# A four-layer decoder trunk: where the first layer's shift and scale vectors are made, and where its squares are summed

## The chip, the cores and the metric

The kernel runs on one core of a Trainium2 chip. The metric is the device time of one execution in microseconds (us); the lower the better. The core has five engines that run side by side, each with its own instruction queue: TensorE (PE, matmuls, with a queue of weight loads shown as PEld), VectorE (DVE), ScalarE (ACT), GpSimd (POOL) and SyncE (SP, which issues most of the transfers). Transfers run on 16 DMA engines.

## The reference

The input x has 256 tokens of 1024 features. Four layers follow each other; each has a token mixer (layer 0: sliding-window attention with 16 query heads and 4 key heads) and a SwiGLU feed-forward part. Ahead of each part x is normed and modulated by vectors that are made from one conditioning vector c:

```python
c_act = jax.nn.silu(c)
for i in range(DEPTH):
    mod = c_act @ ada_w[i] + ada_b[i]          # 1024 -> 6 * 1024
    sh1, sc1, g1, sh2, sc2, g2 = jnp.split(mod, 6, axis=-1)
    h = modulate(rmsnorm(x, norm_gain[i, 0]), sh1, sc1)   # norm * (1 + scale) + shift
    y = swa_mixer(h, ...)                      # by layer: swa, gla, fox, swa
    x = x + g1[:, None, :] * y
    h = modulate(rmsnorm(x, norm_gain[i, 1]), sh2, sc2)
    x = x + g2[:, None, :] * swiglu(h, ffn_w_gu[i], ffn_w_down[i])
return rmsnorm(x, final_norm)
```

So a layer has six vectors of 1024 values, each the product of silu(c) with a 1024 x 1024 matrix of float32. For layer 0 the first two, shift and scale, are needed before anything else can begin.

## The kernel before

x lies with its features on the partitions: 8 tiles k of 128 features by 256 tokens. All matrices are float32. A weight is split into a high and a low part (wh by a cast on ScalarE, L195; wl by a subtraction on VectorE, L197), and so is the normed input (hh, hl). A product of the two is three matmuls (`mm3`, L258): high by high, high by low, low by high.

**The stream of loads.** `items` (L1131) writes one list of all weight transfers, about 1 MB each: "w" items are weights, "a" items are pairs of 128-row tiles of a conditioning matrix. `Stream` (L76) walks it in order. Five raw buffers exist (`RAW`); the transfer of an item is put on SP's queue as soon as the item five places ahead is done, and waits there until the buffer is free. An item is done in two pieces each (`piece`, L99). For layer 0 the order is written out by hand in `ORDER0` (L56): w a weight of the attention, h the shift, s the scale, g the gate of the attention, H and S shift and scale of the feed-forward part, in pairs of tiles. It begins w s h s h s h h w s.

**The conditioning vectors.** `ada_pieces` (L201) makes one tile of 128 values per piece. The matrix lies with outputs on the partitions and the 1024 inputs in a row, and `cact` holds silu(c) on all partitions. One VectorE instruction multiplies, sums along the row and adds the bias (L217). For the tiles that `POOL_ADA` (L60) names, GpSimd multiplies (L212), ScalarE sums the row (L214), and VectorE adds the bias (L215). In layer 0 these are 18 tiles: 5 of the shift, 1 of the scale, 3 of the gate, 5 and 4 of the feed-forward part's shift and scale.

**The first norm.** `first_chunks` (L682) begins layer 0. ScalarE squares the 8 tiles of x (L405), GpSimd adds them up (L416), and a matmul with a column of 1/1024 sums over the partitions (`stat_start` and `stat_end`, L305 to L326; the last tile goes in separately), then the root on ScalarE and the reciprocal y on VectorE (L326). `spread` (L328) puts y onto all partitions, copied as rbs (L694). Then four rounds r follow. Each forces the pairs r of shift and scale, makes A = (1 + scale) * gain (L361), and two tiles of the normed input (`h_tiles`, L426): tk on VectorE (L435), hh on ScalarE with the shift as bias (L437), hl on VectorE (L430). As soon as a weight is ready, the matmuls of the chunk run over the tiles that exist. Chunk 0 (keys, in the PSUM banks "mm") and chunk 1 (values, in the banks "s") are made like this. The value chunk is copied as v by ScalarE (L732), the keys get their rotary position on VectorE (L609 to L612) and GpSimd (L618).

**Behind it.** `swa` (L718) makes four query chunks while a generator, `attn_heads` (L529), is stepped beside them: scores on PE (L544, L545), mask and minimum on VectorE (L572), exponentials on ScalarE (L577), division on ScalarE and VectorE (L557, L558), transposes (L585), the product with the values (L551, L552). GpSimd copies two sink columns for each head (L569, L570). Then comes the output projection and the feed-forward part.

The program's instructions are put into each engine's queue by a scheduler, which keeps the order of the data and may put a later independent instruction ahead of one that it expects to wait.

Of the kernel before, what the change touches and what calls it, by code (L numbers as in the profile page):

```python
# [17 lines left out]
P = 128  # L18
# [16 lines left out]
    ("fin", KT), ("hnorm", 2), ("bgate", GH), ("bf", 1),  # L35
# [20 lines left out]
ORDER0 = "wshshshhwswwwgwwgggSwHSwHSSHHw"  # L56
# [3 lines left out]
POOL_ADA = {(0, 0): (0, 1, 2, 4, 5), (0, 1): (7,), (0, 2): (1, 3, 4), (0, 3): (0, 1, 2, 4, 5), (0, 4): (1, 3, 4, 7)}  # L60
# [83 lines left out]
class Builder:  # L144
# [56 lines left out]
    def ada_pieces(self, it, raw):  # L201

        nc = self.nc
        layer, nt = it[1]
        mod = self.mod[layer]
        bias = self.c("ada_b")[:, layer * 48:(layer + 1) * 48]

        def piece(i):
            w = raw[:, i * D:(i + 1) * D]
            col, b = mod[:, nt + i:nt + i + 1], bias[:, nt + i:nt + i + 1]  # L210
            if (nt + i) % KT in POOL_ADA.get((layer, nt // KT), ()):
                nc.gpsimd.tensor_tensor(out=w, in0=w, in1=self.cact, op=ALU.mult)  # L212
                s = self.t(self.small, [P, 1], "adac", bufs=2)
                nc.scalar.activation(w, w, AF.Copy, accum_out=s)  # L214
                nc.vector.tensor_tensor(out=col, in0=s, in1=b, op=ALU.add)  # L215
            else:
                nc.vector.tensor_tensor_reduce(out=w, in0=w, in1=self.cact, scale=1.0, scalar=b,  # L217
                                               op0=ALU.mult, op1=ALU.add, accum_out=col)
        return [lambda: piece(0), lambda: piece(1)]

# [460 lines left out]

    def first_chunks(self):  # L682

        nc = self.nc
        self.A, self.late = None, []
        self.st.cap = self.st.widx[EARLY]
        self.per_tick = 0.0
        for k in range(KT):
            self.x_done(k)
        self.stat_start(self.acc)  # L690
        self.stat_end()
# [7 lines left out]
        for r in range(4):  # L699
            self.st.force_ada(0, (0, 1), r)  # L700
            self.mod_cols(0, 0, 2 * r, 2 * r + 2, A)
            self.h_tiles(range(2 * r, 2 * r + 2), rbs, A, sh, hh, hl)
            while len(ws) < EARLY and (r == 3 or self.st.pos[f"i0_{len(ws)}"] < self.st.done):
                c = len(ws)
                ws.append([x.rearrange("p (k n) -> p k n", k=KT) for x in self.st.get(f"i0_{c}")])
                self.st.cap = self.st.widx[EARLY]
                outs.append(self.banks(("mm", "s")[c])[0])
                todo.append(0)
            for c, (wh, wl) in enumerate(ws):
                for k in range(todo[c], 2 * r + 2):  # L710
                    for m in range(2):
                        sl = slice(m * P, (m + 1) * P)
                        self.mm3(outs[c][m][:, :S], hh[:, k, sl], hl[:, k, sl], wh[:, k], wl[:, k],
                                 k == 0, k == KT - 1)
                todo[c] = 2 * r + 2
# [483 lines left out]
    def build(self):  # L1199
# [24 lines left out]
        for i in range(2):  # L1224
            ps = self.ps("t")
            sl = slice(i * 512, (i + 1) * 512)
            nc.tensor.matmul(ps, one, crow[:, sl], start=True, stop=True)
            nc.scalar.activation(self.cact[:, sl], ps, AF.Silu)

# [47 lines left out]
def _layout(i):  # L1277
# [5 lines left out]
    a["ada"] = ada.reshape(DEPTH * 6, 4, 2, P, D).transpose(0, 1, 3, 2, 4).reshape(DEPTH * 6, 4, P, 2 * D)  # L1283
    gu = i["ffn_w_gu"].reshape(DEPTH, KT, P, 2, FT, P)[:, :, :, :, :2]
# [30 lines left out]
    put("ones", np.tile(np.array([[1.0 / D, 1.0 / 256]], f), (P, 1)))  # L1315
    put("eps", np.full((P, 1), EPS, f))
# [44 lines left out]
```

## Time and profile before

| | |
|---|---|
| median of 3 runs | 1285.93 us (1284.1 to 1291.37) |
| profiled execution | 1287.15 us, span 1285.4 us |
| PE busy in the span | 1223.3 us (95%) |
| VectorE busy | 1029.2 us (80%) |
| ScalarE busy | 719.4 us (56%) |
| GpSimd busy | 200.5 us (16%) |
| DMA | 298.50 MB, mean 232 GB/s |

The span runs from the first to the last instruction of the program. A row of the view in order of time has start and length in us, engine, line, operation, what is written and read, the shape and a count; brackets give how long the engine was idle before it, and which instruction ended that. A row of the groups has the count, busy time in us and mean in ns of one, then idle time. A row of the waits has the total in us, the number of waits, and the longest. A row of the busy time by stage has the stage, its length, each engine's busy time with its count, the granted clock of TensorE (PEclk), the share of the DMA engines and GB/s.

### The profile page before, as it was taken

How to read it: one execution, taken by the hardware profiler on the slowest of the kernel's cores; microseconds unless marked ns; L12 is line 12 of the kernel's file. 1: busy time of each engine (PE TensorE's matmuls, PEld its weight loads, DVE VectorE, ACT ScalarE, POOL GpSimd, SP SyncE). 2: the span in 40 equal slices, each digit the busy share in tenths (PEclk: the TensorE clock that was granted, in tenths of full speed). 3: DMA queues.
4: the chain of work that ended last, by engine and by line, in shares of the span. 5: the costliest groups of instructions: out<-in, count | busy, mean ns of one | idle time of the engine just before them, and what ended most of it. 6: DMA issues, size and time to landing. Idle time of an engine off the chain costs nothing.

```text
span 1285.4 us, 19492 instructions
## 1 busy us (share of the span) xinstructions
PE 1223.3 (95%) x7284; PEld 1061.3 (83%) x7284; DVE 1029.2 (80%) x1839; ACT 719.4 (56%) x1323; POOL 200.5 (16%) x211
## 2 busy tenths in 40 slices
PE   3698999999999999999999999999999999999997
PEld 2676888888898998888899889888889878888886
DVE  5999998878779889888877657988787977766553
ACT  4567764444576665444448766644445667644442
POOL 5468110001105321000120101100011012000011
PEclk9999999999999999999999999999999999999999
DMA  8665779977744436997875443799777434665450
GB/s 328 256 231 196 267 290 358 340 262 266 264 161 167 165 132 231 352 340 279 271 280 210 157 170 109 275 357 336 273 266 257 168 128 139 222 214 202 161 176 33
DMA packets 44673, 298.50 MB, mean 232 GB/s; under 512 B 5169, under 2 KB 5329, under 8 KB 14242
## 3 DMA queue, kind: packets, MB, share of 16 engines
q1 hardware_dynamic: 43778, 295.53, 63.7%
q8 instruction: 57, 0.93, 0.3%
q10 hardware_dynamic: 432, 1.20, 0.2%
q0 software_dynamic: 368, 0.53, 0.1%
q14 instruction: 38, 0.31, 0.1%
HBM read 296.15 MB, written 1.05 MB: 231 GB/s over the span
## 4 chain that ended last, share of the span: by engine, by line
PE 83%; DVE 9%; ACT 3%; issue 2%; DMA 2%; POOL 1%; DVEq 0%; SPq 0%; POOLq 0%; ACTq 0%
PE mm L1100 13%; PE mm L260 12%; PE mm L261 11%; PE mm L262 11%; PE mm L1102 7%; PE s L260 6%; PE s L261 6%; PE s L262 6%; DVE raw L217 2%; DVE wl L197 2%; PE o L551 2%; PE t L1071 1%; PE s L545 1%; DMA raw<-in_ada 1%; PE t L585 1%
## 5 line engine op out<-in xcount | busy, mean ns | idle before, releaser
L197 DVE TENSOR_TENSOR wl<-raw,wh 128x1024 fp32r<-128x1024 f32 (+2 forms) x408 | 454.6, 1147 | 85.5 <-ACT wh L195 84.3
L195 ACT CAST wh<-raw 128x1024 fp32r<-128x1024 f32 (+2 forms) x408 | 376.5, 963 | 224.2 <-issue 105.9
L1100 PE MATMUL mm<-a,wh 128*128 128x512 f32 x704 | 248.8, 395 | 0.0
L217 DVE CUSTOM_DVE_ANT_0 raw<-raw,cact,const 128x1024 f32<-128x1024 f32 x174 | 230.0, 1337 | 15.3 <-DMA raw<-in_ada 15.3
L260 PE MATMUL mm<-wh,hh 128*128 128x512 f32 (+1 forms) x560 | 200.5, 358 | 20.1 <-ACT hh L437 20.1
L1102 PE MATMUL mm<-a,wl 128*128 128x256 f32 x704 | 199.5, 283 | 0.0
L262 PE MATMUL mm<-wh,hl 128*128 128x512 f32 (+1 forms) x560 | 195.5, 350 | 1.3 <-DVE hl L430 1.3
L261 PE MATMUL mm<-wl,hh 128*128 128x512 f32 (+1 forms) x560 | 195.4, 349 | 0.0
L416 POOL TENSOR_TENSOR sq<-sq,sq 128x256 f32<-128x256 f32 x54 | 59.7, 1105 | 751.2 <-ACT sq L405 731.8
L1100 PEld LDWEIGHTS mm<-a,wh 128*128 128x128 f32 x704 | 132.4, 188 | 29.7
L260 PE MATMUL s<-wh,hh 128*128 128x512 f32 (+2 forms) x384 | 144.7, 378 | 2.9 <-ACT hh L437 2.9
L261 PE MATMUL s<-wl,hh 128*128 128x512 f32 (+2 forms) x384 | 143.0, 373 | 0.2 <-DVE wl L197 0.2
L262 PE MATMUL s<-wh,hl 128*128 128x512 f32 (+2 forms) x384 | 142.2, 374 | 0.0
L260 PEld LDWEIGHTS mm<-wh,hh 128*128 128x128 f32 x560 | 108.4, 194 | 36.2 <-ACT hh L437 21.0
L1102 PEld LDWEIGHTS mm<-a,wl 128*128 128x128 f32 x704 | 132.8, 189 | 0.2
L262 PEld LDWEIGHTS mm<-wh,hl 128*128 128x128 f32 x560 | 107.6, 193 | 14.9 <-DVE hl L430 2.0
L261 PEld LDWEIGHTS mm<-wl,hh 128*128 128x128 f32 x560 | 108.4, 194 | 12.5 <-issue 0.7
L497 DVE SCALAR_TENSOR_TENSOR x<-mm,mod,x 128x256 f32<-128x256 f32 x128 | 61.2, 481 | 44.5 <-PE mm L1102 35.4
L260 PEld LDWEIGHTS s<-wh,hh 128*128 128x128 f32 x384 | 72.5, 189 | 15.3 <-ACT hh L437 3.4
L261 PEld LDWEIGHTS s<-wl,hh 128*128 128x128 f32 x384 | 72.3, 188 | 12.4 <-DVE wl L197 0.5
L262 PEld LDWEIGHTS s<-wh,hl 128*128 128x128 f32 x384 | 71.7, 188 | 12.8
L260 PE MATMUL mm<-oh,wh 128*128 128x256 f32 x256 | 74.7, 297 | 2.6 <-DVE x L497 2.5
(223 smaller groups left out, 2154.6 us busy)
## 6 DMA issues: line engine op xcount, KB each, us to landing
raw<-in_ada SPq DMA_DIRECT2D x96, 1024.0 KB, 6.8
raw<-in_gu SPq DMA_DIRECT2D x88, 1024.0 KB, 6.5
raw<-in_down SPq DMA_DIRECT2D x64, 704.0 KB, 4.9
raw<-in_swa_in SPq DMA_DIRECT2D x12, 1024.0 KB, 5.1
raw<-in_gla_in SPq DMA_DIRECT2D x11, 1024.0 KB, 6.9
raw<-in_fox_in SPq DMA_DIRECT2D x11, 1024.0 KB, 5.3
raw<-in_swa_o SPq DMA_DIRECT2D x8, 1024.0 KB, 5.0
raw<-in_gla_o SPq DMA_DIRECT2D x4, 1024.0 KB, 4.8
```

Of the source, the lines that this page charges most:

```text
L195: nc.scalar.copy(wh[:, sl], raw[:, sl])
L197: eng.tensor_tensor(out=wl[:, sl], in0=raw[:, sl], in1=wh[:, sl].bitcast(F32), op=ALU.subtract)
L217: nc.vector.tensor_tensor_reduce(out=w, in0=w, in1=self.cact, scale=1.0, scalar=b, op0=ALU.mult, op1=ALU.add, accum_out=col)
L260: nc.tensor.matmul(out, ah, bh, start=first, stop=False)
L261: nc.tensor.matmul(out, ah, bl, start=False, stop=False)
L262: nc.tensor.matmul(out, al, bh, start=False, stop=last)
L416: (eng or nc.gpsimd).tensor_tensor(out=q, in0=self.acc, in1=q, op=ALU.add)
L497: self.nc.vector.scalar_tensor_tensor(out=self.x[:, m], in0=ps, scalar=gate[:, m:m + 1], in1=self.x[:, m], op0=ALU.mult, op1=ALU.add)
L545: nc.tensor.matmul(sc[:, P:3 * P], q[:, P:], k, start=True, stop=True)
L551: nc.tensor.matmul(o[rows, :S], v[0], pt[:, :S], start=True, stop=False)
L1100: nc.tensor.matmul(o, wh[:, k], a[:, kk].rearrange("p e n -> p (e n)"), start=kk == 0, stop=False)
L1102: nc.tensor.matmul(o[:, S:], wl[:, k], a[:, kk, 0], start=False, stop=kk == FT - 1)
```

## The change

The shift vector of layer 0's first norm is made by TensorE: the first 1024 columns of `ada_w[0]` lie in memory with the inputs on the partitions, two tiles of outputs per transfer, as before 1 MB each. Eight accumulating matmuls with silu(c) as columns (`ccol`, new, made by eight matmuls and one activation at the start) give one row of 256 values in PSUM; ScalarE copies it, two small matmuls turn it into two columns, and VectorE adds the bias (`ada_rows`). The turn is queued when the round's scale tiles have been queued. All other conditioning vectors are made by VectorE alone, so that the 18 products of GpSimd and their sums on ScalarE are gone. The squares of x are no longer added on GpSimd: PE takes the sum over partitions of every square and adds it up in PSUM (`stat_all`). The list of loads begins h s w h s h s w h s in place of w s h s h s h h w s, and the first weight is taken up in round 0.

```diff
-    ("fin", KT), ("hnorm", 2), ("bgate", GH), ("bf", 1),
+    ("fin", KT), ("hnorm", 2), ("bgate", GH), ("bf", 1), ("one", 1),
...
-ORDER0 = "wshshshhwswwwgwwgggSwHSwHSSHHw"
+ORDER0 = "hswhshswhswwwgwwgggSwHSwHSSHHw"
...
-POOL_ADA = {(0, 0): (0, 1, 2, 4, 5), (0, 1): (7,), (0, 2): (1, 3, 4), (0, 3): (0, 1, 2, 4, 5), (0, 4): (1, 3, 4, 7)}
...
+        if layer == 0 and nt < KT:
+            return self.ada_rows(mod[:, nt:nt + 2], bias[:, nt:nt + 2], raw)
+
         def piece(i):
             w = raw[:, i * D:(i + 1) * D]
             col, b = mod[:, nt + i:nt + i + 1], bias[:, nt + i:nt + i + 1]
-            if (nt + i) % KT in POOL_ADA.get((layer, nt // KT), ()):
-                nc.gpsimd.tensor_tensor(out=w, in0=w, in1=self.cact, op=ALU.mult)
-                s = self.t(self.small, [P, 1], "adac", bufs=2)
-                nc.scalar.activation(w, w, AF.Copy, accum_out=s)
-                nc.vector.tensor_tensor(out=col, in0=s, in1=b, op=ALU.add)
-            else:
-                nc.vector.tensor_tensor_reduce(out=w, in0=w, in1=self.cact, scale=1.0, scalar=b,
-                                               op0=ALU.mult, op1=ALU.add, accum_out=col)
+            nc.vector.tensor_tensor_reduce(out=w, in0=w, in1=self.cact, scale=1.0, scalar=b,
+                                           op0=ALU.mult, op1=ALU.add, accum_out=col)
         return [lambda: piece(0), lambda: piece(1)]
+
+    def ada_rows(self, mod, bias, raw):
+
+        nc = self.nc
+        w = raw[:, :2048].rearrange("p (k n) -> p k n", k=KT)
+        ps = self.ps("o")
+        row = self.t(self.small, [P, S], "fc", bufs=2)[:1]
+
+        def product():
+            for k in range(KT):
+                nc.tensor.matmul(ps[:1, :S], self.ccol[:, k:k + 1], w[:, k], start=k == 0, stop=k == KT - 1)
+            nc.scalar.copy(row, ps[:1, :S])
+
+        def turn():
+            for m in range(2):
+                nc.tensor.matmul(ps[:, S + m:S + m + 1], row[:, m * P:(m + 1) * P], self.c("one")[:1],
+                                 start=True, stop=True)
+            nc.vector.tensor_tensor(out=mod, in0=ps[:, S:S + 2], in1=bias, op=ALU.add)
+        return [product, lambda: self.turns.append(turn)]
...
+    def stat_all(self):
+
+        nc = self.nc
+        self.stat = [self.ps("t"), self.ps("t")]
+        for k in range(KT):
+            q = self.t(self.small, [P, S], "sq", bufs=4)
+            nc.scalar.activation(q, self.x[:, k], AF.Square)
+            if k == KT - 1:
+                self.last_sq = q
+                break
+            for b in range(NB):
+                nc.tensor.matmul(self.stat[b][:, :1], q[:, b * P:(b + 1) * P],
+                                 self.c("ones")[:, 0:1], start=k == 0, stop=False)
+        self.stat_end()
+
     def first_chunks(self):
 
         nc = self.nc
-        self.A, self.late = None, []
         self.st.cap = self.st.widx[EARLY]
         self.per_tick = 0.0
-        for k in range(KT):
-            self.x_done(k)
-        self.stat_start(self.acc)
-        self.stat_end()
+        self.turns = []
+        self.stat_all()
...
             self.st.force_ada(0, (0, 1), r)
+            self.turns.pop()()
             self.mod_cols(0, 0, 2 * r, 2 * r + 2, A)
             self.h_tiles(range(2 * r, 2 * r + 2), rbs, A, sh, hh, hl)
-            while len(ws) < EARLY and (r == 3 or self.st.pos[f"i0_{len(ws)}"] < self.st.done):
+            while len(ws) < EARLY and (r % 3 == 0 or self.st.pos[f"i0_{len(ws)}"] < self.st.done):
                 c = len(ws)
+                if r == 0 and c:
+                    break
...
+        ps = self.ps("o")
+        for k in range(KT):
+            nc.tensor.matmul(ps[:, k:k + 1], crow[:, k * P:(k + 1) * P], one[:, :1], start=True, stop=True)
+        self.ccol = self.t(self.small, [P, KT], "ccol", bufs=1)
+        nc.scalar.activation(self.ccol, ps[:, :KT], AF.Silu)
...
+    a["ada"][0] = _chunks(i["ada_w"][0, :, :D], 256)
...
+    put("one", np.ones((P, 1), f))
```

The tag "o" has one PSUM bank, the tag "fc" two buffers, "sq" four.

## The prediction

> **What bounds the kernel now.** I read the busy time by stage first, then the waits and the chain of the first 55 us, then the rows in order of time there, then the groups of the stage behind it. Only layer 0 is touched: 0 to 55 us makes its first norm and two projection chunks, 55 to 145 us holds its attention and output projection, the rest is untouched.
>
> ```profile
> core 0: us, PE busy (x) PEld busy (x) DVE busy (x) ACT busy (x) POOL busy (x), PEclk, DMA share, GB/s
> 0.00:55.00 55.00, 23.92 (x112) 19.38 (x113) 38.40 (x59) 23.47 (x42) 24.97 (x22) 1.00 0.79 302
> 55.00:145.00 90.00, 81.43 (x533) 65.36 (x532) 87.90 (x196) 64.97 (x160) 53.69 (x51) 0.97 0.61 226
> 145.00:1285.00 1140.00, 1117.99 (x6644) 976.51 (x6643) 902.93 (x1586) 630.96 (x1123) 121.81 (x140) 0.99 0.64 229
> ```
>
> PE is busy for 1118.0 of the last 1140 us, but idle for 31.1 of the first 55 us and 8.6 of the next 90 us: those two numbers cap what this change can win. In the first stage VectorE works 38.4 us and does hardly anything before 14.87 us, so it has no room left there.
>
> ```profile
> by line: DVE raw L217 28.8%; DMA raw<-in_ada 16.1%; issue 10.2%; DMA x<-in_x 10.0%; DVE hl L430 8.3%; POOL sq L416 7.1%; DVE wl L197 6.5%; DVE A L361 4.5%; DVE tk L435 4.1%; PE t L309 1.8%; PE t L322 1.6%; ACT sq L405 1.3%; ACT hh L437 0.9%
> PE mm L260 <- ACT hh L437: 20.1, 3, 9.0
> 14.62 5.63 POOL L212 TENSOR_TENSOR raw<-raw,cact 128x1024 f32<-128x1024 f32 x2 [2.00 <-DMA raw<-in_ada]
> 14.87 0.17 DVE L326 RECIPROCAL y<-sd 128x2 f32<-128x2 f32 x1 [13.88 <-ACT sd L325]
> 15.01 3.04 DVE L217 CUSTOM_DVE_ANT_0 raw<-raw,cact,const 128x1024 f32<-128x1024 f32 x1
> 17.97 3.36 DVE L217 CUSTOM_DVE_ANT_0 raw<-raw,cact,const 128x1024 f32<-128x1024 f32 x1
> 24.66 1.28 DVE L217 CUSTOM_DVE_ANT_0 raw<-raw,cact,const 128x1024 f32<-128x1024 f32 x1
> 50.26 0.16 DVE L215 TENSOR_TENSOR mod<-adac,const 128x1 f32<-128x1 f32 x1
> 51.72 0.89 DVE L430 SCALAR_TENSOR_TENSOR hl<-tk,mod,hh 128x256 fp32r<-128x256 f32 x2 [0.18 <-ACT hh L437]
> 54.96 0.37 ACT L732 COPY v<-s 128x256 f32<-128x256 f32 x1 [0.99 <-PE s L262]
> ```
>
> The first line is the chain's share by line up to 55 us: the adaLN products on VectorE (L217) lead it, and PE waits 20.1 us for the normed tiles hh. The rows below say why. A product of 1024 columns costs VectorE 1.28 us alone (24.66) and 3.04 to 3.36 us while GpSimd runs its own (14.62 to 20.25): the two engines do not run such operations at once, one stands until the other is through. So the work given to GpSimd is not free to VectorE. The last shift column is there at 50.42 us and the last low half hl at 52.61 us; the second chunk's copy v starts at 54.96 us. I measure the first stage by these two ends.
>
> **The change, first stage: VectorE's own list.**
>
> ```profile
> L217 DVE CUSTOM_DVE_ANT_0 raw<-raw,cact,const 128x1024 f32<-128x1024 f32 x10 | 20.6, 2079 | 0.0
> L197 DVE TENSOR_TENSOR wl<-raw,wh 128x1024 fp32r<-128x1024 f32 x4 | 4.7, 1218 | 0.0
> L435 DVE SCALAR_TENSOR_TENSOR tk<-rbs,A,x 128x256 f32<-128x256 f32 x8 | 3.5, 482 | 0.1
> ```
>
> The groups of the first 55 us: ten products at 2079 ns become eight at 1.28 us (all scale tiles; tile 7 comes over from GpSimd, shift tiles 3, 6 and 7 go to PE): 10.2 us. The rest stays: splits 4.7, tk 3.5, hl 8 x 0.44 = 3.5 (from the 51.72 row), four A and four shift additions at 0.16 = 1.3. That is 23.2 us. From 14.87 us without a wait it ends at 38.1 us.
>
> Loads. The shift and scale vectors with the two weight chunks are ten transfers of 1 MB, in five buffers.
>
> ```profile
> 1.56 5.50 DMA x<-in_x
> GB/s 0 93 231 407 441 417 435 411 429 429 423 429 411 412 273 0 149 399 435 393 429 423 125 334 375 209 411 131 0 0 0 71 340 429 405 369 292 357 346 411
> const<-in_const ACTq DMA_DIRECT2D x1, 656.0 KB, 6.6
> ```
>
> At the full slices' 420 to 430 GB/s 1.05 MB takes 2.45 us. Behind x (7.06 us), ten of them and the second constants (1.6 us) end at 33.2 us; two products (2.56) and what follows the last column now (50.26 to 52.61, 2.35) end at 38.1 us. The row also shows slices at 0 between 38 and 43 us: the queue stood there for a buffer. The new order puts shift 0 ahead of scale 0 ahead of weight 0; every queue behind SP's is in that order, and a buffer whose product is late holds all later loads. No other queue gains or loses a load.
>
> PE's new list: per round of two shift tiles, 8 matmuls of 256 columns into one row, two turns of the row into columns; per square, two matmuls; eight matmuls for the column form of c.
>
> ```profile
> 3.27 0.33 PEld L1227 LDWEIGHTS t<-hh,fc 1*128 1x128 f32 x1 [0.52 <-issue]
> 4.12 0.33 PEld L1227 LDWEIGHTS t<-hh,fc 1*128 1x128 f32 x1 [0.52 <-issue]
> 2.28 3.75 PE L1227 MATMUL t<-hh,fc 1*128 1x512 f32 x4 [2.28 <-DMA hh<-in_c]
> 12.68 1.01 PE L309 MATMUL t<-const,sq 128*128 128x1 f32 x4 [6.65 <-POOL sq L416]
> 13.55 0.99 PE L322 MATMUL t<-const,sq 128*128 128x1 f32 x4
> 15.09 1.22 PE L332 MATMUL t<-const,y 128*128 128x128 f32 x4 [0.55 <-DVE y L326]
> 154.90 0.61 PE L309 MATMUL t<-const,sq 128*128 128x1 f32 x4 [0.60 <-POOL sq L416]
> 73.80 0.43 PE s L545 x2
> 37.81 0.42 PE L261 MATMUL mm<-wl,hh 128*128 128x256 f32 x1
> 38.03 0.42 PE L260 MATMUL mm<-wh,hh 128*128 128x256 f32 x1
> 44.19 0.58 PE L260 MATMUL mm<-wh,hh 128*128 128x256 f32 x1 [3.82 <-ACT hh L437]
> 48.40 0.29 PE L261 MATMUL s<-wl,hh 128*128 128x256 f32 x1
> 48.52 0.28 PE L262 MATMUL s<-wh,hl 128*128 128x256 f32 x1
> ```
>
> An f32 matmul is two passes (four rows for two calls). Early, a 512-column pass takes 0.85 us (3.27 to 4.12), so one of 256 columns 0.43 us, and later 0.215 us (0.43 for two): 16 passes are 6.8 us at the early pace and 3.4 us at the late one. The projection's own matmuls show the same two paces: 0.22 us from start to start at 38 us, 0.12 us at 48 us. The PEclk column says 1.00 in both, so the pace has to be read from the starts. The fast pace begins only after PE has been kept busy from 44.19 to about 48 us, 3.8 us.
>
> Squares: 32 passes at 0.2 us (L309 to L322: 0.87 for four) are 6.5 us early, at 0.12 us (154.90) 3.8 us. They stand behind 16 passes for c, 3.3 us or less from 6.03 us on. So the sums end at 12 to 16.4 us against 14.54 us now, where GpSimd's six additions were on the chain: a change of -2.5 to +1.9 us, taken as -0.3 (14.2 us), and it is hidden while VectorE has its two products to do. The spread over partitions (L332 and its root) follows 1.8 us later: 16.0 us for the first product of PE.
>
> A round of PE is then product, copy of the row by ScalarE (0.4, as v's 0.37), two turns (four short passes, 0.4 to 1.0), the bias on VectorE (0.16). The PSUM bank is single, so the next product waits for that bias; 12 projection matmuls lie between (2.6 or 1.4 us). At the late pace: 3.4 + 0.4 + 0.6 + 0.2 = 4.6; the fourth bias ends at 16.0 + 4 x 4.6 + 3 x 1.4 = 38.6 us, hl 2.2 us later at 40.8 us. VectorE's list and the loads both give 38.1 us, so PE's chain is last, by little: 52.6 - 40.8 = **11.8 us won**, and up to 14.5 if the chain overlaps better. Two waits are new. VectorE's bias addition waits for PE's turns, and behind it stand A, tk, hl and the next split; ScalarE's row copy waits for PE's product, and behind it stand hh and the casts. Both are counted in the round. ScalarE loses its six accumulating passes over GpSimd's products here and gains four short copies.
>
> The Trainium skill's page TensorE: Matmul & The Clock Gate (HAM oscillation) says that PE bursts parted by waits longer than its activity window of about 3.4 us fall back to half speed, each time anew. The trace agrees as to the two paces; by that rule the rounds would be dear, and the price is the second rival below.
>
> **The change, second stage.** Twelve products (three gate, five and four of the second norm) move from GpSimd to VectorE. The groups are those of 55 to 130 us, GpSimd's that of 0 to 135 us.
>
> ```profile
> L197 DVE TENSOR_TENSOR wl<-raw,wh 128x1024 fp32r<-128x1024 f32 x14 | 24.1, 1760 | 0.0
> L558 DVE TENSOR_SCALAR pr<-pr,rd 128x256 f32<-128x256 f32 x14 | 17.0, 1218 | 0.0
> L215 DVE TENSOR_TENSOR mod<-adac,const 128x1 f32<-128x1 f32 x7 | 4.3, 625 | 0.0
> 97.38 0.35 DVE L558 TENSOR_SCALAR pr<-pr,rd 128x256 f32<-128x256 f32 x1
> L212 POOL TENSOR_TENSOR raw<-raw,cact 128x1024 f32<-128x1024 f32 x18 | 48.5, 2704 | 5.9 <-ACT raw L214 2.9 <-DMA raw<-in_ada 2.0 <-issue 0.9
> ```
>
> It adds 12 x 1.28 = 15.4 us to VectorE. It takes away the additions (4.3) and the time that VectorE stood for GpSimd: L558 17.0 - 14 x 0.35 = 12.1, L197 24.1 - 14 x 1.22 = 7.0 us, together 19.1 us, some 3 of it owed to the rotary additions that stay on GpSimd. So 20 go and 15 come: VectorE gets 5 us lighter. PE idles only 8.6 us of this stage, and a product now sits as one piece in front of softmax steps in VectorE's queue, where PE's transposes wait for it. I take half, **2.5 us won**, with -8.6 and +5 as the ends.
>
> The sum: 11.8 + 2.5 = 14.3 us. The profiled execution of 1287.15 us (span 1285.4) becomes 1272.9; it lies 1.2 us over the median, 1285.93, so the median becomes **1271.6 us**. From 145 us on nothing moves but the start.
>
> **Rivals.** A measurement of this kernel can tell about 0.5%, 6.4 us, from no change.
>
> First, the second stage gives back: the twelve products fall on the softmax chain in full and hold GpSimd's small copies too.
>
> ```profile
> 112.25 1.25 POOL L570 COPY sm<-nsink 128x1 f32<-128x1 f32 x1
> 113.56 0.18 POOL L570 COPY sm<-nsink 128x1 f32<-128x1 f32 x1
> ```
>
> The 0.18 us copy took 1.25 us beside a product on VectorE; no waits of ScalarE on these copies are listed now, which speaks against. It costs +5 in place of -2.5: 1279 us. Chance 0.10.
>
> Second, PE cools in every round: 3.8 us of each product at the early pace, the rest at the late one, 5.3 us in all, a round 6.9 us, with 2.0 between: 18.2 + 4 x 6.9 + 3 x 2.0 = 51.8 us against 50.4 now. The first stage wins nothing and the second 2.5: about 1285 us. For it: the burst at 37 us stayed slow. Against: a product alone outlasts the 3.8 us of work that brought the fast pace. Chance 0.12.
>
> Third, the slower side: PE becomes the bound at the early pace throughout, its queue being in order, with each product behind the projection matmuls of the round before, which wait for hl. A round is 6.8 + 0.4 + 1.0 + 0.2 = 8.4 us, between rounds 2.6 + 1.8; from 18.2 us the fourth bias ends at 18.2 + 33.6 + 13.2 = 65.0 us, 14.6 late; less 2.5, 1298 us. It decides from the point where a round exceeds (50.4 - 18.2) / 4 = 8 us. Chance 0.06.
>
> That the change doesn't reach what it says I count out: GpSimd's products are gone from the code, not moved behind a condition.
>
> **How the numbers follow.** The forecast has 0.72, first rival 0.10, second 0.12, third 0.06. The forecast's own range is 1263 (14.5 and 8.6 won) to 1279 (7 won in all, half of each term); with the first rival, its first term as low as 9, it reaches 1282, and the two hold 0.82. Faster by over 0.5% is the forecast and most of the first rival, 0.79; within it the second rival and the rest, 0.15; slower 0.06.
>
> **What would show it.** In the new profile no GpSimd row multiplies raw by cact; VectorE's products read 1.2 to 1.3 us from the first on; the last hl before the second chunk ends near 41 us and the value copy near 43 us instead of 54.96; passes of the row products start 0.215 us apart from the second round on; from 55 to 130 us L558 has a mean under 0.6 us. Row products 0.43 us apart in all rounds, or a scale product that waits for SP's loads past 36 us, would make the first term wrong; L558 or the exponentials waiting behind products would make the second wrong.

## The result, and the profile after

The kernel after takes 1292.51 us in the median of 13 runs (1290.06 to 1294.46), the kernel before 1286.86 us in its 13 (1284.1 to 1292.38). The ratio of the runs is 1.0033, with a 95% interval of 1.0019 to 1.0047: the change costs about 4.2 us (0.33% of 1286.86; 2.4 to 6.0 by the interval), where 14.3 us had been forecast as won. That is less than the 0.5% set as the bound of "no change", and outside the forecast's range. The profiled execution of after, 1294.46 us with a span of 1292.7, is the longest of its 13, so single profiles are compared below by their places in time and not by their ends.

Five places of the two profiles show where it went:

| | before, us | after, us | forecast, us |
|---|---|---|---|
| last shift column added | 50.42 | 53.84 | 38.6 |
| last low half hl ends | 52.61 | 55.91 | 40.8 |
| value copy v starts | 54.96 | 59.45 | 43 |
| last head cast to its high half oh | 135.63 | 131.92 | |
| ninth of the 16 updates of x by the output projection | 142.22 | 149.12 | |

The first stage was to win 11.8 us and loses 3.3. From there to the last head after is 7.0 us shorter, and from the last head to the ninth update 10.6 us longer (17.2 in place of 6.6). Part of both is work that changed sides: when the last head comes, after has begun three of the 16 updates, before six. What the two add up to, 3.6 us, doesn't depend on that. Nor is 3.3 us exact to the tenth: e1 and e8 below, whose edits leave the first stage as it is in after, have their last pair of hl at 54.52 and 53.68 us, after at 55.02, before at 51.72; so the loss is 2.0 to 3.3 us.

The rows of the last head and the ninth update, of before with PE's waits from 130 to 150 us, and of after:

```profile
135.63 0.37 ACT L493 CAST oh<-o 128x256 fp32r<-128x256 f32 x1
142.22 0.48 DVE L497 SCALAR_TENSOR_TENSOR x<-mm,mod,x 128x256 f32<-128x256 f32 x1
PE mm L260 <- DVE x L497: 2.3, 1, 2.3
```

```profile
131.92 0.37 ACT L508 CAST oh<-o 128x256 fp32r<-128x256 f32 x1 [0.95 <-PE o L567]
149.12 0.47 DVE L512 SCALAR_TENSOR_TENSOR x<-mm,mod,x 128x256 f32<-128x256 f32 x1
```

The busy time by stage of after comes first; the three stages are those shown of before.

```profile
0.00:55.00 55.00, 45.63 (x194) 29.03 (x195) 21.78 (x45) 16.18 (x32) 1.93 (x9) 0.94 0.76 292
55.00:145.00 90.00, 82.79 (x540) 66.51 (x538) 77.01 (x203) 52.76 (x133) 22.89 (x38) 0.96 0.60 217
145.00:1285.00 1140.00, 1123.55 (x6667) 979.45 (x6667) 907.58 (x1595) 632.30 (x1125) 122.92 (x140) 0.99 0.64 230
```

In the first stage PE and VectorE changed places: PE (the first busy column) goes from 23.92 to 45.63 us, VectorE (the third) from 38.40 to 21.78. The relief of VectorE is there, and in the second stage more than was forecast (87.90 to 77.01); the time is not.

Next, PE's rows of the first stage in order of time: start, length, line; L708 and L337 are the squares, L226 the row product, L347 the spread of y, L231 the turn, L275 to L277 the projection.

```profile
9.85 6.13 PE L708 MATMUL t<-const,sq 128*128 128x1 f32 x28 [0.57 <-ACT sq L703]
15.85 0.99 PE L337 MATMUL t<-const,sq 128*128 128x1 f32 x4
16.77 3.57 PE L226 MATMUL o<-raw,ccol 128*1 128x256 f32 x8
20.27 1.22 PE L347 MATMUL t<-const,y 128*128 128x128 f32 x4
21.42 2.27 PE L226 MATMUL o<-raw,ccol 128*1 128x256 f32 x8
24.14 0.60 PE L231 MATMUL o<-const,fc 1*128 1x1 f32 x4 [0.45 <-ACT fc L227]
27.53 0.51 PE L275 MATMUL mm<-wh,hh 128*128 128x256 f32 x2 [2.78 <-ACT wh L194]
28.79 0.39 PE L276 MATMUL mm<-wl,hh 128*128 128x256 f32 x1 [0.76 <-DVE wl L196]
...
31.02 4.31 PE L226 MATMUL o<-raw,ccol 128*1 128x256 f32 x16
...
36.70 1.02 PE L226 MATMUL o<-raw,ccol 128*1 128x256 f32 x4 [0.32 <-DVE mod L233]
...
39.29 2.75 PE L226 MATMUL o<-raw,ccol 128*1 128x256 f32 x12
...
48.04 4.33 PE L226 MATMUL o<-raw,ccol 128*1 128x256 f32 x16
```

And of VectorE in the same stretch the four additions that end a round (L233), with the work that leads to the second, and the last hl:

```profile
17.30 1.28 DVE L213 CUSTOM_DVE_ANT_0 raw<-raw,cact,const 128x1024 f32<-128x1024 f32 x1
...
24.85 0.16 DVE L233 TENSOR_TENSOR mod<-o,const 128x2 f32<-128x2 f32 x1 [5.05 <-PE o L231]
...
27.51 2.36 DVE L196 TENSOR_TENSOR wl<-raw,wh 128x1024 fp32r<-128x1024 f32 x2 [0.45 <-ACT wh L194]
...
36.49 0.16 DVE L233 TENSOR_TENSOR mod<-o,const 128x2 f32<-128x2 f32 x1 [3.50 <-PE o L231]
...
43.25 0.16 DVE L233 TENSOR_TENSOR mod<-o,const 128x2 f32<-128x2 f32 x1 [2.73 <-PE o L231]
...
53.68 0.16 DVE L233 TENSOR_TENSOR mod<-o,const 128x2 f32<-128x2 f32 x1 [3.81 <-PE o L231]
...
55.02 0.89 DVE L445 SCALAR_TENSOR_TENSOR hl<-tk,mod,hh 128x256 fp32r<-128x256 f32 x2 [0.18 <-ACT hh L452]
```

Every addition now waits for PE, 15.1 us in all. The first is at 24.85, the rounds after it take 11.6, 6.8 and 10.4 us. Look at the second product. The addition before it ends at 25.01 and frees its bank; it starts at 31.02. In those 6.0 us PE stood for the weight's high half wh (2.78) and its low half wl (0.76), and then ran the rest of 12 projection matmuls. They are ahead of the product in the queue. The fourth product starts 4.6 us after its bank is free (43.41 to 48.04), again behind projection matmuls; of the third, four passes go at once and the rest wait for 12 matmuls.

PE also ran at half speed for part of this: the granted clock (the third figure from the end) was 0.51 and 0.50 in two stretches of 3.4 us, in which the second and the fourth product begin.

```profile
29.00:32.40 3.40, 3.40 (x14) 2.26 (x14) 3.37 (x6) 0.00 (x0) 0.00 (x0) 0.51 0.74 277
46.20:49.50 3.30, 3.30 (x14) 2.08 (x13) 3.30 (x5) 0.00 (x0) 0.00 (x0) 0.50 0.93 360
```

Last, VectorE behind the last head (L512 updates x, L213 is a product):

```profile
132.67 0.48 DVE L512 SCALAR_TENSOR_TENSOR x<-mm,mod,x 128x256 f32<-128x256 f32 x1
133.06 1.27 DVE L213 CUSTOM_DVE_ANT_0 raw<-raw,cact,const 128x1024 f32<-128x1024 f32 x1
...
134.26 1.28 DVE L213 CUSTOM_DVE_ANT_0 raw<-raw,cact,const 128x1024 f32<-128x1024 f32 x1
...
135.47 1.28 DVE L213 CUSTOM_DVE_ANT_0 raw<-raw,cact,const 128x1024 f32<-128x1024 f32 x1
...
136.67 0.48 DVE L512 SCALAR_TENSOR_TENSOR x<-mm,mod,x 128x256 f32<-128x256 f32 x1
...
140.68 0.48 DVE L512 SCALAR_TENSOR_TENSOR x<-mm,mod,x 128x256 f32<-128x256 f32 x1
...
144.69 0.48 DVE L512 SCALAR_TENSOR_TENSOR x<-mm,mod,x 128x256 f32<-128x256 f32 x1
...
148.56 0.48 DVE L512 SCALAR_TENSOR_TENSOR x<-mm,mod,x 128x256 f32<-128x256 f32 x1
```

Three products of 1.2 us stand in front of each update, so updates come 4.0 us apart: 3 x 1.2 + 0.4. Ten products run here, from 133.06 us on, the last done at 146.4. By the order of the loads five of them are moved ones. In before GpSimd starts its last product at 126.92 us, ahead of the last head, and VectorE has only its own five here, from 130.50 to 139.47, two of them behind the last head. PE waits for a free bank each time, 6.5 us in all against 2.3 in before; from the waits of 130 to 150 us:

```profile
PE mm L275 <- DVE x L512: 6.5, 5, 2.3
```

### The profile page after: what moved, and what is told of

The parts are those of the page before. It is cut to its first block, busy times and chain, and to the rows that moved or that the text cites. A ratio compares the mean times of both kernels' runs of the same rounds, so it can differ in the third digit from the quotient of the medians.

```text
span 1292.7 us, 19668 instructions
## 1 busy us (share of the span) xinstructions
PE 1252.8 (97%) x7404; PEld 1075.6 (83%) x7404; DVE 1007.9 (78%) x1845; ACT 703.0 (54%) x1292; POOL 147.7 (11%) x187
## 4 chain that ended last, share of the span: by engine, by line
PE 86%; DVE 6%; ACT 3%; issue 2%; POOL 1%; DMA 1%; DVEq 0%; POOLq 0%; ACTq 0%
PE mm L1130 12%; PE mm L275 12%; PE mm L276 11%; PE mm L277 11%; PE s L275 7%; PE s L276 7%; PE s L277 7%; PE mm L1132 6%; PE o L566 2%; DVE wl L196 2%; PE s L560 2%; PE o L226 1%; PE t L600 1%; PE t L1101 1%; PE s L559 1%
## 5 line engine op out<-in xcount | busy, mean ns | idle before, releaser
L196 DVE TENSOR_TENSOR wl<-raw,wh 128x1024 fp32r<-128x1024 f32 (+2 forms) x408 | 448.5, 1132 | 85.9 <-ACT wh L194 84.7
L213 DVE CUSTOM_DVE_ANT_0 raw<-raw,cact,const 128x1024 f32<-128x1024 f32 x184 | 234.6, 1292 | 13.2 <-DMA raw<-in_ada 13.2
L275 PE MATMUL mm<-wh,hh 128*128 128x512 f32 (+1 forms) x560 | 198.2, 355 | 3.4 <-ACT wh L194 2.8
L1132 PE MATMUL mm<-a,wl 128*128 128x256 f32 x704 | 196.6, 279 | 0.0
L277 PE MATMUL mm<-wh,hl 128*128 128x512 f32 (+1 forms) x560 | 194.1, 347 | 0.0
L275 PE MATMUL s<-wh,hh 128*128 128x512 f32 (+2 forms) x384 | 144.8, 378 | 3.3 <-ACT hh L452 2.9
L431 POOL TENSOR_TENSOR sq<-sq,sq 128x256 f32<-128x256 f32 x48 | 55.6, 1159 | 756.8 <-ACT sq L420 738.0
L277 PE MATMUL s<-wh,hl 128*128 128x512 f32 (+2 forms) x384 | 142.1, 374 | 0.0
L275 PEld LDWEIGHTS mm<-wh,hh 128*128 128x128 f32 x560 | 106.2, 190 | 19.7 <-issue 4.0
L276 PEld LDWEIGHTS mm<-wl,hh 128*128 128x128 f32 x560 | 106.5, 190 | 14.6 <-DVE wl L196 2.1
L277 PEld LDWEIGHTS mm<-wh,hl 128*128 128x128 f32 x560 | 106.5, 190 | 13.6 <-issue 0.8
L512 DVE SCALAR_TENSOR_TENSOR x<-mm,mod,x 128x256 f32<-128x256 f32 x128 | 61.3, 480 | 47.1 <-PE mm L1132 37.9
L275 PEld LDWEIGHTS s<-wh,hh 128*128 128x128 f32 x384 | 72.1, 188 | 16.0 <-ACT hh L452 3.4
L277 PEld LDWEIGHTS s<-wh,hl 128*128 128x128 f32 x384 | 71.6, 188 | 13.1
L275 PE MATMUL mm<-oh,wh 128*128 128x256 f32 x256 | 75.6, 301 | 6.6 <-DVE x L512 6.5
```

What stands on the lines that cost most here:

```text
L196: eng.tensor_tensor(out=wl[:, sl], in0=raw[:, sl], in1=wh[:, sl].bitcast(F32), op=ALU.subtract)
L275: nc.tensor.matmul(out, ah, bh, start=first, stop=False)
L276: nc.tensor.matmul(out, ah, bl, start=False, stop=False)
L277: nc.tensor.matmul(out, al, bh, start=False, stop=last)
L431: (eng or nc.gpsimd).tensor_tensor(out=q, in0=self.acc, in1=q, op=ALU.add)
L512: self.nc.vector.scalar_tensor_tensor(out=self.x[:, m], in0=ps, scalar=gate[:, m:m + 1], in1=self.x[:, m], op0=ALU.mult, op1=ALU.add)
```

## The experiments

**The theory** has two parts. (a) In the first stage the chain moved from VectorE to PE's queue, and its length is set by what stands ahead of each row product there: projection matmuls that wait for wh, wl and hh. (b) In the second stage the attention gains from the absence of GpSimd's products, but the output projection loses more, because ten products now stand on VectorE in front of its updates of x. **The rivals**: the pace of the passes themselves, or the squares on PE, make the first stage long; loads held by late products make it long; the second stage only carries on what the first lost. The runs of before taken beside these kernels have medians of 1288.33 us (e1 to e4), 1288.55 (e5, e7, e8) and 1288.88 (e10 to e12); each ratio is to those beside it.

### Second stage: twelve products given back to GpSimd (e1)

```diff
+POOL_ADA = {(0, 2): (1, 3, 4), (0, 3): (0, 1, 2, 4, 5), (0, 4): (1, 3, 4, 7)}
...
+            if (nt + i) % KT in POOL_ADA.get((layer, nt // KT), ()):
+                nc.gpsimd.tensor_tensor(out=w, in0=w, in1=self.cact, op=ALU.mult)
...
```

> The changed kernel with the twelve products of the gate and of the second norm's shift and scale back on GpSimd; shift on TensorE, squares in PSUM and the load order stay. My theory (loss in two places: 3.3 us in the rounds of the first norm, about 10 us in the output projection, where ten products in a row stand ahead of the x updates; the attention between them wins 4 to 7 us): the last hl still ends near 56 us, no x update waits for products, the ninth x update comes near 146 us against 142.7 before and 149.6 after; time 1288 to 1290, between the two. Rival (the whole loss is made in the first stage): ninth x update and time as after, 1292.

1288.88 us, ratio 1.0005 (0.9985 to 1.0025). The last hl pair starts at 54.52 us, the last head comes at 143.05 and the ninth update at 147.24: from head to update 4.2 us in place of 17.2, while the attention loses the gain (11.1 us later). The hl and the time are as foretold; the update is 1.2 us later. The interval is wide: it allows 0.25% over before.

### Second stage: the same move in the kernel before (e2)

```diff
-POOL_ADA = {(0, 0): (0, 1, 2, 4, 5), (0, 1): (7,), (0, 2): (1, 3, 4), (0, 3): (0, 1, 2, 4, 5), (0, 4): (1, 3, 4, 7)}
+POOL_ADA = {(0, 0): (0, 1, 2, 4, 5), (0, 1): (7,)}
```

> The kernel before, with only the twelve products of the second stage moved to VectorE; the first stage is untouched. My theory: last hl at 52.6 us as before, attention 4 us quicker, then products in a row ahead of the x updates of the output projection; ninth x update 4 to 7 us later than before, time 1290 to 1293. Rival (GpSimd's products only stood in VectorE's way, the forecast's second term): ninth x update 2 to 5 us earlier, time 1282 to 1285.

1290.74 us, ratio 1.0027 (1.0009 to 1.0044). The hl pair starts at 51.57 (before 51.72), the last head comes at 130.93, 4.7 us earlier, and the ninth update at 148.12, 5.9 us later. From the waits of 125 to 150 us of this kernel:

```profile
PE mm L260 <- DVE x L497: 7.1, 5, 2.3
```

So the move of the twelve products is slower by itself, by 0.27%, with the first stage untouched: part (b) holds, and "carries on what the first lost" falls.

### First stage: the squares back on GpSimd (e3)

```diff
-        self.stat_all()
+        self.A, self.late = None, []
+        for k in range(KT):
+            self.x_done(k)
+        self.stat_start(self.acc)
+        self.stat_end()
```

> The changed kernel with the squares of x added on GpSimd as before. My theory: the sums are no earlier, since the squares start behind the activation that makes the column form of c (9.4 us) in both; sums end at 16.5 to 17 us, last hl within 1 us of 55.9, time within 2 us of after. Rival (32 passes on TensorE hold up the first product and all that follows): the first bias 2 to 3 us earlier than 24.85 us, last hl near 53 us, time 1289 to 1290.

1290.17 us, ratio 1.0021 (1.0004 to 1.0039). The first product starts at 16.94 us (after 16.77) and the first addition at 25.04 (24.85): where the squares are added delays neither. The expectation for the last hl is missed all the same: its pair starts at 51.77, 3.3 us earlier than after, with rounds of 8.0, 7.2 and 10.1 us. That is nearer the rival's 53 us, but the rival's cause, a first addition 2 to 3 us earlier, is not there. In this kernel ScalarE casts the first weight at 24.18, ahead of hh, and VectorE splits it at 25.50, so the projection matmuls in front of the second product are through by 28.3 instead of 31.0, and its 16 passes take 3.61 us. The scheduler's order changed with the edit, which speaks for the queue and was not what this run was made for.

### First stage: the product ahead of the projection (e4)

```diff
-ORDER0 = "hswhshswhswwwgwwgggSwHSwHSSHHw"
+ORDER0 = "hswhshshwswwwgwwgggSwHSwHSSHHw"
...
-            self.turns.pop()()
+            if r == 0:
+                self.st.force(self.st.pos["i0_0"])
+            self.turns.pop(0)()
+            if r < 3:
+                self.st.force(next(i for i, it in enumerate(self.st.items) if it[1] == (0, 2 * r + 2)))
...
+            with self.tc.issue_after(self.last_mm.ins):
```

The next round's product is queued right behind the turn, this round's projection matmuls behind that product; the first weight is split before the first turn, and the addition keeps its place in VectorE's program.

> The changed kernel with the next round's row product queued on TensorE ahead of this round's projection matmuls, weight 0 split in VectorE's idle time ahead of the first bias, and the second weight loaded behind the last shift pair. My theory (rounds are long because the product stands behind the projection matmuls in the queue): biases about 6 to 7 us apart instead of 11.6, 6.8 and 10; last hl at 45 to 48 us instead of 55.9; time 5 to 9 us under after, 1284 to 1288. Rival (loads and buffers set the rounds): last hl not before 53 us, time within 2 us of after.

1287.27 us, ratio 0.9991 (0.9976 to 1.0006). PE of this kernel in the third round:

```profile
34.78 3.61 PE L226 MATMUL o<-raw,ccol 128*1 128x256 f32 x16 [0.32 <-DVE mod L233]
...
39.94 0.60 PE L231 MATMUL o<-const,fc 1*128 1x1 f32 x4
...
40.87 3.61 PE L226 MATMUL o<-raw,ccol 128*1 128x256 f32 x16 [0.32 <-DVE mod L233]
```

The product starts 0.3 us after the addition ahead of it and takes 3.61 us; twelve projection matmuls that wait for nothing run between it and its turn, and the round is 6.1 us, as the prediction had it (4.6 + 1.4). The three rounds are 7.8, 6.1 and 8.8. The hl pair starts at 51.72, not at 45 to 48. The first addition is at 26.80, now behind the weight's split (24.52 to 26.88 on VectorE), and the product of the second round takes 5.30 us, in part at the early pace; the fourth addition stands on VectorE behind a wl that waits 1.98 us for its cast and behind two products: VectorE's order took over from PE's.

### First stage: three quarters of the product left out (e10)

The row product takes two of its eight tiles of c; this leaves out three quarters of each shift sum.

```diff
-            for k in range(KT):
+            for k in (0, KT - 1):
                 nc.tensor.matmul(ps[:1, :S], self.ccol[:, k:k + 1], w[:, k], start=k == 0, stop=k == KT - 1)
```

> The kernel after, with the row products of the shift vector cut to two of their eight tiles of c (4 passes of TensorE in place of 16); three quarters of each shift sum are left out of the computation. Theory (the serial row of TensorE's work sets the first stage): the first product falls from 6.9 us to about 1.7, the others from 4.3 to about 1.1, so the shift additions come 4 to 5 us earlier in the first round and about 3 us each in the second and fourth, and the last low half hl starts at 43 to 47 us in place of 55.90. Rival (loads held by buffers, or the casts and splits of the weights, set it whatever the products take): the last hl stays at 51 us or later. The second stage keeps its ten products in a row on VectorE, so the time falls by no more than the first stage does: a single run of 1280 to 1286 us by the theory, 1288 or more by the rival.

One run: 1288.92 us, in the rival's band. The groups of the row product in the first stage, of after and of this kernel:

```profile
L226 PE MATMUL o<-raw,ccol 128*1 128x256 f32 x64 | 18.3, 442 | 0.3 <-DVE mod L233 0.3
```

```profile
L226 PE MATMUL o<-raw,ccol 128*1 128x256 f32 x16 | 6.6, 559 | 0.3 <-DVE mod L233 0.3
```

11.7 us of passes are gone, and the last hl pair starts at 49.22, only 5.8 us earlier. That is between the two expectations. The additions are 10.0, 4.0 and 10.1 us apart. In the two long rounds PE waits for wl (24.59 to 26.95 on VectorE) and for hh (4.00 us before 39.17), runs 12 projection matmuls, and only then the four passes. VectorE has a part in the second of them: it runs two products (35.36 to 37.85 us) ahead of the A and tk that this hh waits for. So the passes' own time is worth about half of itself; the rest lies in what stands ahead of the product and in what those matmuls wait for. The second stage is as in after (17.2 us from head to update), as was foretold.

### First stage: the projection behind the fourth round (e11)

```diff
-            for c, (wh, wl) in enumerate(ws):
+            for c, (wh, wl) in enumerate(ws if r == 3 else ()):
```

> The kernel after, with all projection matmuls of the two early chunks issued behind the fourth round, so that no product stands behind them in TensorE's queue. Theory (the place in the queue, not the pace, made the rounds 11.6, 6.8 and 10.4 us long): each product starts within 0.5 us of the shift addition before it, the rounds fall to 7 to 8.5 us even where the passes keep the early pace of 0.43 us, and the last hl starts at 49 to 52 us. Rival (the early pace itself, with TensorE cooled in every round): passes stay 0.43 us apart, rounds of 9 us or more, last hl at 54 us or later. The value copy comes some 10 us behind the last hl, since 96 matmuls are then left to do, so the time does not fall: 1290 to 1296 us.

One run: 1288.72 us; the time is a little under the 1290 to 1296 expected. The hl pair starts at 51.89. PE and VectorE of this kernel, two views:

```profile
27.78 0.58 PE L276 MATMUL mm<-wl,hh 128*128 128x256 f32 x1 [0.72 <-DVE wl L196]
28.29 6.26 PE L226 MATMUL o<-raw,ccol 128*1 128x256 f32 x16
...
36.47 3.62 PE L226 MATMUL o<-raw,ccol 128*1 128x256 f32 x16
```

```profile
23.84 0.16 DVE L233 TENSOR_TENSOR mod<-o,const 128x2 f32<-128x2 f32 x1 [4.10 <-PE o L231]
...
35.86 0.16 DVE L233 TENSOR_TENSOR mod<-o,const 128x2 f32<-128x2 f32 x1 [4.59 <-PE o L231]
...
41.39 0.16 DVE L233 TENSOR_TENSOR mod<-o,const 128x2 f32<-128x2 f32 x1 [0.91 <-PE o L231]
...
50.56 0.16 DVE L233 TENSOR_TENSOR mod<-o,const 128x2 f32<-128x2 f32 x1 [1.75 <-PE o L231]
```

The rounds are 12.0, 5.5 and 9.2 us, not 7 to 8.5: the scheduler still put three matmuls ahead of the second product, which wait for wh (2.79 us) and wl (0.72), and 4.1 us of them ahead of the fourth. Only in the middle round does nothing ahead of the product wait: five matmuls run there, the product starts 0.5 us after the addition's end and the round is 5.5 us. The second round is long for two reasons at once, 4.3 us in the queue and a product of 6.26 us at mostly the early pace, so here the rival has its share.

### Second stage: five products to GpSimd, the product ahead (e7)

```diff
+POOL_ADA = {(0, 3): (2, 4, 5), (0, 4): (4, 7)}
```

Beside it stand the edits of e4.

> The kernel of e4 with five of the sixteen products of the second norm's shift and scale back on GpSimd (shift tiles 2, 4, 5, scale tiles 4, 7), all of them among the ten that come last. My theory: from the last head to the ninth x update 9 to 12 us instead of 17.3, time 2 to 5 us under e4, 1282 to 1285. Rival (GpSimd's products hold VectorE as long as VectorE's own): still 16 to 18 us, time as e4, 1287.

1283.39 us, ratio 0.9957 (0.9942 to 0.9972). The last head is where e4 has it (126.61 to 126.56), the ninth update at 139.95 in place of 143.75: 13.3 us between, not 9 to 12, but the time is as expected.

### Second stage: another order of the products (e8 alone, e5 with the product ahead)

Tiles of the feed-forward part's vectors (S, H) are taken earlier, between the heads, so that two products are left behind the last head.

```diff
-ORDER0 = "hswhshswhswwwgwwgggSwHSwHSSHHw"
+ORDER0 = "hswhshswhswwwgwgSwgSgHSwHSHwHw"
```

> The changed kernel with only the order of the loads behind weight 4 changed as in e5; the rounds of the first norm stay as they were. My theory: last hl near 56 us as after; from the last head to the ninth x update 6 to 9 us instead of 17.3; time 1283 to 1286, that is 7 to 9 us under after, and faster than before by 1 to 4 us. Rival (the loss in the output projection is TensorE's cooled clock or the later loads, not the place of the products): 15 us or more stay there, time 1290 to 1293.

1288.74 us, ratio 1.0003 (0.999 to 1.0017), so it missed its 1283 to 1286. From head to update it is 7.6 us in place of 17.2, but the last head comes at 138.99, 7.1 us later than in after: of 9.6 us won behind the head, 7.1 are lost ahead of it, where the products now run.

> The kernel of e4 (row product ahead, weight 0 split early) with another order of the loads behind weight 4: w g w g S w g S g H S w H S H w H w in place of g w w g g g S w H S w H S S H H w, so that two products and not ten are left behind the last attention head; all products stay on VectorE. My theory (the ten products between the last head and the x updates are the second stage's loss): from the last low half of the heads to the ninth x update 6 to 9 us instead of 17.3; ninth x update 8 to 10 us ahead of the kernel before; time 1278 to 1281. Rival (the twelve products cost VectorE their time wherever they stand): the attention gets longer by what the projection wins, ninth x update within 3 us of e4's, time 1286 to 1288.

With the edits of e4 too: 1283.35 us, ratio 0.9961 (0.9941 to 0.9980), 2.4 us above the top of the expectation and under its rival's 1286 to 1288. The ninth update is 1.8 us ahead of before, not 8 to 10. Last head 132.87 (e4 126.56), ninth update 140.42 (e4 143.75): of 9.6 us won behind the head, 6.3 are paid ahead of it.

### All three edits together (e12)

> The kernel with the product ahead of the projection in TensorE's queue and the new tail of the order by hand, and five of the second stage's products given to GpSimd (three of the scale items and two of the last shift items). Alone the tail gave 3.9 us and the five products 3.9 us over the product ahead alone. If they are the same gain, a row of products in front of VectorE's x updates, taken away twice, the two together give 1282 to 1284 us, ratio 0.995 to 0.997. If each takes away another part, they add: 1278 to 1281 us, ratio 0.992 to 0.994.

1280.8 us, ratio 0.9946 (0.9925 to 0.9967): the fastest kernel here, 0.54% under before. From the busy time of the output projection, of after and of this kernel (after the length stand the busy times of PE, its weight load, VectorE, ScalarE and GpSimd, then the granted clock):

```profile
140.00:145.00 5.00, 2.93 (x12) 2.64 (x12) 5.00 (x10) 4.29 (x5) 0.00 (x0) 0.50 0.99 388
```

```profile
140.00:145.00 5.00, 5.00 (x45) 5.00 (x44) 4.06 (x10) 2.71 (x6) 0.60 (x1) 1.00 0.60 218
```

PE is busy throughout in place of 2.93 of 5 us, at the full clock; four updates of x fall into this stretch in place of two. Whether the two edits of the second stage add or take away the same loss stays open: the median lies with "they add", the ratio between the two bands, and the interval overlaps those of e5 and e7. Its ninth update, at 141.85, is not earlier than theirs.

## Why the prediction was wrong, point by point

**What bounded the kernel** was read rightly: VectorE at 3 us a product beside GpSimd. What was said of the speed of VectorE's instructions came true. Its products read 1.28 us from the first on, no GpSimd row multiplies by cact, and L558 (now L573) fell to a mean of 354 ns:

```profile
L573 DVE TENSOR_SCALAR pr<-pr,rd 128x256 f32<-128x256 f32 x16 | 5.6, 354 | 0.0
```

**The step that failed** is the PE round of the first stage, "3.4 + 0.4 + 0.6 + 0.2 = 4.6" with "3 x 1.4" between, from 16.0 to 38.6 us. The last addition ended at 53.84, 15.2 us late. The terms:
- The first product starts at 16.77 (0.8 late) and ends at 23.7, not 19.4: its first eight passes are at the early pace (3.57 us), and the spread, 1.2 us, stands in the middle of it. The first addition is 4.4 us late.
- The three rounds behind it take 28.8 us and not 18.0. Of the 10.8 us, 7.8 lie in the queue: 6.0 and 4.6 us from a free bank to the product, where 1.4 had been put. It had been counted as 12 matmuls' run, but those matmuls also wait: for hh, for the cast of the weight behind it on ScalarE, for the split on VectorE. Some of them run at half clock, too (0.21 us apart from 29 us on in place of 0.12). The passes are 4.31, 3.77 and 4.33 us against 3.4: another 2.2. At full pace throughout they take 3.6 (e4); the rest is the half clock of the two stretches above.
- That the number 6.0 for a round is right where nothing in front of the product waits is shown by e4 (6.1) and e11 (5.5, with nine projection matmuls in the round in place of 12). That PE's queue holds the chain is shown by e4 and e10. No run reached 41 us: in e4 VectorE's own order is next, and the last hl ends at 52.6.

**The rival that came closest** is the third, "each product behind the projection matmuls of the round before", and with it the threshold of 8 us a round: the mean is 9.6. It had 0.06. Its price, 14.6 us late, was too high since the pace was not early throughout. The second rival, PE cooling in every round, has a share: the clock fell in two rounds of the three, and that is in the 2.2 us above. Neither rival's time is the measured one. The prediction saw the queue's order, and gave the chance to the other case without a reason from the profile: the trace of before shows such matmuls in front of nothing on PE, but it shows their waits, 20.1 us for hh (the quoted line of the waits), and all of that can stand in front of a product.

**Squares.** The sums end at 16.8 us, not 14.2, just outside the 12 to 16.4. The 32 passes take 7.0 us, which is what 0.87 us for four gives; the 6.5 of the prediction was too small for its own row. e3 has the sums no earlier, with GpSimd's additions behind ccol's activation on ScalarE, so it cost nothing to add them on PE. But in both kernels the first product stands in PE's queue behind the sums, and its matrix, issued at 2.02 us, landed 8.2 us later, at 10.2; the product starts at 16.77. No run has it ahead of the sums.

**Loads.** VectorE's list and the loads were both put at 38.1 us. From SP's waits of the first 70 us of after:

```profile
SPq L181 <- PE o L226: 28.8, 4, 13.4
```

A buffer is held until PE has read it, as foretold, and the DMA queue stands. It held up no product in after: the four pairs of the shift land at 10.2, 17.7, 28.9 and 40.4 us, each at least 6.5 us before its product starts (16.77, 31.02, 36.70 and 48.04), and the two weights at 15.2 and 35.0, their casts starting at 26.44 and 42.40. So the rival "loads held by late products" falls for the first stage of after.

**Second stage: -2.5 us.** It came to +3.6 (6.9 late at the ninth update, of which 3.3 were there before). Up to the last head 7.0 us were won, more than "-20 + 15.4" gives, since only seven of the 12 moved products, and three updates fewer, had run by then. What the sum lacks is a place: it took the 12 products as spread through the stage, and five of them, with five that VectorE had before, fall behind the last head, where 12 us on VectorE have only the output projection beside them. The first rival had this as +5, a price near the measured one, and the mechanism elsewhere: it put it on the softmax and on the sink copies.

**The sum.** +3.3 and +3.6 are 6.9 us in one profile; the 13 runs say 2.4 to 6.0. By e2 (+0.27%) and e1 (+0.05%, -0.15 to +0.25) most of the loss is the second stage's move. But e4, which repairs the first stage and has all that move, is 0.42% under after, some 5.4 us, where its last hl is 3.3 us earlier; its last head is 5.4 us earlier. So the two parts do not add: e1 and e2 alone put the ninth update 5.0 and 5.9 us late, both together 6.9. The last hl was not the best end to measure the first stage by. The last head follows the value copy v by 72.0 to 73.2 us in after, e4, e3 and e11 (v at 59.45, 54.53, 56.56 and 56.69, head at 131.92, 126.56, 129.73 and 129.90; 75.0 in e10 and 76.1 in e2), and v of e4 is 4.9 us earlier than that of after: this nearly gives its 5.4. In e3 and e11, with hl as early as in e4 but v at 56.6, the head is only 2 us earlier. Why e1, with its hl 2.8 us and its ninth update 5.0 us late, is no slower than before in the median stays open.

## What to carry to other kernels

Work moved to an engine with an in-order queue costs what stands ahead of it there, waits included: write that queue down, with the wait of every entry, before taking the work's own time as its price. Taking work from an engine that holds another one up helps where that other was stretched (here VectorE beside GpSimd), and hurts where the other must now do all of it in a row; so ask of each moved instruction at which time it will run, not only in which stage. The mean of a stage (here VectorE 11 us lighter in the second) can fall while the stage gets longer.

## What the runs showed of the hardware that was not expected

The fast pace of PE came after 3.8 us of work in before. In after PE had been busy from 9.85 us on without a pause, with squares of one column 0.22 us apart for 7 us, and the eight passes of 256 columns behind them still ran 0.43 us apart; the fast pace came among the next eight (2.27 us from 21.42 on). In e3, with PE idle until 15.14, it came no later (12 passes from 19.89 take 3.99 us). In e11, with the same instructions as after up to there, it came over 1 us earlier than in after, so the moment varies from run to run:

```profile
20.16 0.71 PE L347 MATMUL t<-const,y 128*128 128x128 f32 x4
```

Those four matmuls took 1.22 us in after. So the one-column passes did not seem to count as work; no run here tests that alone. The Trainium skill's page TensorE: Matmul & The Clock Gate, in its part on the HAM clock gate, says that about 3.4 us of sustained activity release the clock; here 7 us of one-column passes did not.

The clock also fell without a long wait. In after PE waits 2.3, 1.9 and 1.1 us for the updates of x, and its matmuls go from 0.12 to 0.21 us apart; the first of a group reads 0.58 us in place of 0.39:

```profile
137.21 0.39 PE L275 MATMUL mm<-oh,wh 128*128 128x256 f32 x1 [2.32 <-DVE x L512]
...
141.22 0.58 PE L275 MATMUL mm<-oh,wh 128*128 128x256 f32 x1 [1.92 <-DVE x L512]
...
145.23 0.58 PE L275 MATMUL mm<-oh,wh 128*128 128x256 f32 x1 [1.08 <-DVE x L512]
```

The granted clock is 0.50 from 140 to 145 us (the row above). In the first stage it fell at 29 us behind waits of 2.78 and 0.76 us, parted by two matmuls. The same page's section HAM oscillation tells of waits longer than its window of about 3.4 us; none here is as long. It costs nothing in this place, since 12 matmuls at half speed still end before the next update.
